# A planner that counts work on upper partitions, and activations with a scale per partition, as longer

## The chip, the cores and the metric

The kernel runs on one core of one Trainium2 chip. The metric is the device time of one execution in microseconds (us), the median over runs. The traces shown are of one profiled execution.

## What is computed

A trunk of two encoder layers over 512 tokens of 1024 features, in float32. Each layer is four residual steps, each followed by a layer norm:

```python
for i in range(DEPTH):                                   # DEPTH = 2
    y = swiglu(x, ffn_w_gate[i, 0], ffn_w_up[i, 0], ffn_w_down[i, 0])
    x = layer_norm(ALPHA * x + 0.5 * y, ln_g[i, 0], ln_b[i, 0])
    if i % 2 == 0:
        y = mixer_ab(x, ab_w_in[j], ab_w_out[j], ab_q_gain[j], ab_k_gain[j], ab_sink[j], ang_2d, ang_1d)
    else:
        y = mixer_c(x, c_w_in[j], c_w_out[j], c_rpb[j])
    x = layer_norm(ALPHA * x + y, ln_g[i, 1], ln_b[i, 1])
    y = memory_attn(x, mem, mem_w_q[i], mem_w_kv[i], mem_w_o[i])
    x = layer_norm(ALPHA * x + y, ln_g[i, 2], ln_b[i, 2])
    y = swiglu(x, ffn_w_gate[i, 1], ffn_w_up[i, 1], ffn_w_down[i, 1])
    x = layer_norm(ALPHA * x + 0.5 * y, ln_g[i, 3], ln_b[i, 3])
```

Mixer A/B (layer 0) has 8 heads A of dense attention and 8 heads B of attention in a window of 128 tokens to each side with a sink logit, all of width 64, and one output projection. Mixer C (layer 1) has 16 heads of width 64, each query attending to a neighbourhood of 8 x 16 tokens on a grid, with a bias by relative position. The memory step has 4 heads of width 256 over 256 memory tokens.

## The kernel before

The program is written as a plain sequence of operations, but is not issued in that order. A recorder (`Graph`) stands in for the five engines. It notes each operation with its engine, the operations it depends on, the buffers it uses, and `ns`, the time that `Graph.cost` thinks it takes. `Graph.emit` then runs a list scheduler, `Graph.plan`, twice: it keeps a clock for each engine and always issues the ready operation with the smallest key on the engine that is free first. In the first pass the key is the written order. From the first plan `deadlines` works out when each operation must start at the latest so that TensorE is not held up, and in the second pass these due times are the keys of VectorE, ScalarE and GpSimd. Nothing of these times reaches the chip; they set only the order of the instructions in each engine's queue. Every engine works off its queue in order. All operations are called from one helper, so nearly all instructions have the line L154 in the profile.

Buffers come in classes with a fixed number each, and a tile waits for its class to have one free: `t2` 14, `slab` 27, `raw` 2 (weights as they arrive), and the PSUM banks `a` 3 (projections, scores), `d` 2 (outputs), `t` 3 (transposes). Names in an order are the tile's class and running numbers.

Float32 products are made of two or three matmuls on a rounded high part and a remainder. So each operand is split: ScalarE writes the rounded copy (CAST, COPY or ACTIVATE), VectorE the difference (TENSOR_TENSOR or SCALAR_TENSOR_TENSOR).

In mixer A/B, `queries` splits transposed queries of two heads at a time: for each head, ScalarE writes the high part into one half of the partitions, and VectorE the remainder into the other half; both are 64 partitions high, and of each at least one operand lies on partitions 64 to 127 in VectorE's case, every second one in ScalarE's. For each of the 16 heads the loop then takes scores (`a`), their extreme (`mn`: TENSOR_REDUCE for A, an ISA instruction for B), the exponential with its sum (`l`), a RECIPROCAL, and `normalise`, a ScalarE copy whose scale is a column with a value per partition; the weights are transposed (`t`), split (`slab`), and multiplied with the values (`d`). Beside the last heads run the first half of the output projection (`x` += `d`) and the loads of its weights (`raw`<-ab_w_out).

In mixer C, `attend` moves the output's upper 64 partitions by a ScalarE COPY and adds on VectorE, 64 high, per head. Keys and queries are laid out by DMA (`slab`<-`t`), issued by SyncE in a queue which also loads weights (`raw`<-c_w_in). Each head is normalised in four pieces by `normalise`. The memory step uses `normalise` too.

`Graph.extent` gives the partitions that an operand covers, from its first to its last.

Of the kernel before, what the change touches and what calls it, by code (L numbers as in the profile page):

```python
# [65 lines left out]
class Graph:  # L66
# [45 lines left out]
    @staticmethod  # L112
    def cost(engine, method, out, ins, kw):
        n = 1
        for d in (out if method != "tensor_reduce" else ins[0]).ap[1:]:
            n *= d[1]
        wide = any(z.space == bass.MemoryType.PSUM for z in ins + [out]) if engine != "sync" else False
        if method == "dma_start":
            return 1200.0 if "accum_op" in kw else 600.0
        if engine == "tensor":  # L120
            return max(n / 2.4 + 14, 111)
        scalars = sum(1 for z in ins if z.ap[-1][1] == 1)
        if engine == "vector":
            if method == "tensor_scalar" and not wide:
                n = n / 2
            return n / 0.96 + 72 + 60 * scalars + 120 * (method == "scalar_tensor_tensor" and "accum_out" in kw)
        if engine == "scalar":
            return n / 1.2 + (55 if wide else 100) + 45 * scalars + 130 * ("accum_out" in kw)
        if n <= 8:
            return 270.0 if method == "tensor_scalar" else 200.0 if method != "tensor_tensor" else 390.0 + 157.0 * n  # L130
        if method == "memset":
            return n * 0.83 + 60
        dense = len(ins) == 2 and all(z.ap[-1][0] != 0 for z in ins)
        return n * (2.4 if dense else 1.7) + (70 if dense else 130)
# [1494 lines left out]
```

## Time and profile before

| | |
|---|---|
| runs | 2140.82, 2141.06, 2138.66 us; median 2140.82 |
| the profiled execution | 2139.44 us, span of its trace 2137.6 us |
| TensorE (PE) busy | 2116.6 us, 99% |
| weight loads (PEld) | 1886.3 us, 88% |
| VectorE (DVE) | 1725.9 us, 81% |
| ScalarE (ACT) | 1150.2 us, 54% |
| GpSimd (POOL) | 288.1 us, 13% |
| granted TensorE clock | 0.998 of full |

Times in a trace count from the start of the span. Mixer A/B lies at about 330 to 545 us, mixer C at about 1400 to 1600 us. A row of the timeline has the start, the length (of several instructions in a run, from the first start to the last end), the engine, the line, the operation, output and inputs, and how many; in brackets stands how long the engine was idle before it and what ended that. PE is TensorE's matmul, PEld its weight load, SPq the queue of SyncE. Matmuls are pipelined, so their rows overlap, and a row lasts longer than the step from one matmul to the next.

### The profile page before, as it was taken

Reading aid. Unit: us, or ns where it says so; the run is one execution under the profiler, and the core shown is the slowest. Engines: PE = TensorE matmul, PEld = TensorE weight load, DVE = VectorE, ACT = ScalarE, POOL = GpSimd, SP = SyncE. Lnnn points to the kernel's source line nnn. Section 1 sums busy time; section 2 is a strip of 40 time slices with the busy share of each in tenths; the row PEclk is TensorE's granted clock in tenths of the full one; section 3 lists DMA queues with packets and bytes.
Section 4 is the critical chain, followed back from the end, with each engine's and each line's share of the span. In section 5 each row is a group of like instructions: output and inputs, shape, how many; then the busy total and the mean of one; then the engine's idle time right before and its main releaser. Section 6 shows DMA issues by size and latency. Waiting matters only on the chain.

```text
span 2137.6 us, 33130 instructions
## 1 busy us (share of the span) xinstructions
PE 2116.6 (99%) x12904; PEld 1886.3 (88%) x12904; DVE 1725.9 (81%) x2460; ACT 1150.2 (54%) x1863; POOL 288.1 (13%) x379
## 2 busy tenths in 40 slices
PE   9999999999999999999999999999999999999997
PEld 7999988788888899999889999888888888999996
DVE  7789989888748879998879999865568479699997
ACT  5555543798446555445545455456665455445552
POOL 0001015310002000000200000412110011000003
PEclk9999999999999999999999999999999999999999
DMA  6566562003443247564445556255354333456551
GB/s 203 142 165 144 139 188 88 21 17 103 138 138 109 83 115 188 148 153 133 139 108 140 127 139 190 72 168 153 104 163 156 127 102 99 109 148 150 140 155 60
DMA packets 208861, 275.96 MB, mean 129 GB/s; under 512 B 10688, under 2 KB 151616, under 8 KB 208704
## 3 DMA queue, kind: packets, MB, share of 16 engines
q1 hardware_dynamic: 175904, 221.14, 33.3%
q0 software_dynamic: 32512, 52.44, 13.7%
q8 instruction: 102, 1.67, 0.3%
q14 instruction: 55, 0.45, 0.1%
q10 hardware_dynamic: 288, 0.26, 0.0%
HBM read 259.12 MB, written 4.19 MB: 123 GB/s over the span
## 4 chain that ended last, share of the span: by engine, by line
PE 72%; DMA 1%; DVE 1%; ACT 1%; SPq 0%; issue 0%; DVEq 0%; ACTq 0%
PE a L154 45%; PE d L154 15%; PE t L154 11%; DMA slab<-t 1%; DVE slab L154 1%; ACT t L154 0%; DVE x L154 0%; SPq L154 0%; DMA raw<-c_w_in 0%; DMA raw<-ab_w_out 0%; ACT slab L154 0%; DVE t L154 0%; DVE xl L154 0%; ACT junk L154 0%; DVEq L1625 0%
## 5 line engine op out<-in xcount | busy, mean ns | idle before, releaser
L154 DVE TENSOR_TENSOR slab<-slab,slab 128x1024 fp32r<-128x1024 f32 (+3 forms) x638 | 728.6, 1168 | 74.9 <-ACT slab L154 35.8
L154 ACT CAST slab<-slab 128x1024 fp32r<-128x1024 f32 (+2 forms) x498 | 472.3, 983 | 338.9 <-DVE slab L154 141.5
L154 PE MATMUL a<-slab,slab 128*128 128x256 f32 (+2 forms) x2456 | 570.5, 315 | 3.9 <-DMA slab<-t 3.4
L154 PE MATMUL a<-xh,slab 128*128 128x256 f32 (+2 forms) x2480 | 560.2, 315 | 0.1
L154 PEld LDWEIGHTS a<-slab,slab 128*128 128x128 f32 x2456 | 417.2, 191 | 37.4 <-issue 2.7
L154 PE MATMUL d<-slab,slab 128*128 128x512 f32 (+2 forms) x1856 | 447.8, 382 | 0.8 <-DVE slab L154 0.5
L154 PEld LDWEIGHTS a<-xh,slab 128*128 128x128 f32 x2480 | 416.9, 191 | 33.6 <-ACT slab L154 1.0
L154 PE MATMUL a<-xl,slab 128*128 128x256 f32 (+1 forms) x1240 | 390.6, 315 | 0.0
L154 PE MATMUL a<-raw,slab 128*128 128x256 f32 x2048 | 388.9, 283 | 0.9 <-DVE t L154 0.7
L154 PEld LDWEIGHTS d<-slab,slab 128*128 128x128 f32 x1856 | 329.2, 189 | 57.6 <-DVE slab L154 1.2
L154 PEld LDWEIGHTS a<-raw,slab 128*128 128x128 f32 x2048 | 328.1, 192 | 6.4 <-ACT slab L154 1.7
L154 PEld LDWEIGHTS a<-xl,slab 128*128 128x128 f32 x1240 | 236.6, 191 | 18.1
L154 PE MATMUL t<-slab,slab 128*128 128x512 f32 (+1 forms) x864 | 209.6, 383 | 0.0
L154 DVE TENSOR_TENSOR slab<-raw,slab 128x1024 fp32r<-128x1024 f32 (+2 forms) x132 | 158.6, 1220 | 23.7 <-ACT slab L154 23.6
L154 PEld LDWEIGHTS t<-slab,slab 128*128 128x128 f32 x864 | 151.4, 189 | 25.1
L154 DVE TENSOR_TENSOR slab<-t,slab 128x512 fp32r<-128x512 f32 (+2 forms) x211 | 131.4, 642 | 29.0 <-ACT slab L154 27.8
L154 ACT CAST slab<-raw 128x1024 fp32r<-128x1024 f32 (+1 forms) x124 | 123.0, 1021 | 25.7 <-PE a L154 9.0
L154 ACT CAST slab<-t 128x512 fp32r<-128x512 f32 (+2 forms) x211 | 114.4, 567 | 41.5 <-PE t L154 13.7
L154 DVE SCALAR_TENSOR_TENSOR x<-d,x 128x512 f32<-128x512 f32 x168 | 114.8, 686 | 18.8 <-PE d L154 18.0
L154 ACT COPY t<-a 128x512 f32<-128x512 f32 x96 | 56.3, 587 | 125.0 <-PE a L154 71.9
L154 POOL DMA_DIRECT2D slab<-ffn_w_down x40 | 47.7, 1193 | 313.5 <-DVE slab L154 291.2
L154 PE MATMUL a<-slab,xh 128*128 128x512 f32 (+1 forms) x272 | 79.8, 375 | 0.5 <-ACT xh L154 0.5
(126 smaller groups left out, 2138.2 us busy)
## 6 DMA issues: line engine op xcount, KB each, us to landing
slab<-ffn_w_gate SPq DMA_DIRECT2D x80, 512.0 KB
slab<-ffn_w_up SPq DMA_DIRECT2D x80, 512.0 KB
slab<-ffn_w_down SPq DMA_DIRECT2D x80, 512.0 KB
slab<-ffn_w_down POOLq DMA_DIRECT2D x40, 512.0 KB, 5.6
raw<-mem_w_kv SPq DMA_DIRECT2D x16, 1024.0 KB
slab<-t SPq DMA_DIRECT2D x96, 128.0 KB
slab<-ffn_w_gate POOLq DMA_DIRECT2D x16, 512.0 KB, 7.8
slab<-ffn_w_up POOLq DMA_DIRECT2D x16, 512.0 KB, 5.8
```

What stands on the lines that cost most here:

```text
L154: op.call = lambda: fn(*args, **kw)
```

## The change

`Graph.cost` gets two terms. `aside` adds 120 ns to an operation on VectorE or ScalarE of which any operand starts on a partition above 0. `scaled` adds 42 ns to a ScalarE activation whose scale is a tensor.

```diff
         scalars = sum(1 for z in ins if z.ap[-1][1] == 1)
+        aside = 120.0 * any(Graph.extent(z)[0] > 0 for z in ins + [out])
         if engine == "vector":
             if method == "tensor_scalar" and not wide:
                 n = n / 2
-            return n / 0.96 + 72 + 60 * scalars + 120 * (method == "scalar_tensor_tensor" and "accum_out" in kw)
+            return n / 0.96 + 72 + aside + 60 * scalars + 120 * (method == "scalar_tensor_tensor" and "accum_out" in kw)
         if engine == "scalar":
-            return n / 1.2 + (55 if wide else 100) + 45 * scalars + 130 * ("accum_out" in kw)
+            scaled = 42 * hasattr(kw.get("scale"), "tensor")
+            return n / 1.2 + (55 if wide else 100) + aside + 45 * scalars + 130 * ("accum_out" in kw) + scaled
```

The terms meet the operations of `queries` and `attend` named above, and every `normalise`. For an operation 512 wide that reads PSUM the plan's time goes from 605 to 725 ns on VectorE and from 482 to 602 on ScalarE; for a `normalise` of 512 columns it goes from 572 to 614 ns.

The program has the same instructions before and after; only their order on each engine differs, nearly all of it within mixer A/B from about 380 us on and mixer C. Line numbers move from L154 to L156.

First place, head A, near 439 to 446 us. On VectorE, before: `slab_790` are the half-high remainders of queries, `mn_782` and `mn_786` the extremes of scores, `slab_794` the split of a transposed bank, `slab_824` that of a weight.

```order
L154 SCALAR_TENSOR_TENSOR slab_790_871<-t_789_870,slab_790_871 64x512 x2
L154 TENSOR_REDUCE mn_782_863<-a_781_862 128x1
L154 TENSOR_REDUCE mn_786_867<-a_785_866 128x1
L154 RECIPROCAL l_776_857<-l_776_857 128x1
L154 RECIPROCAL l_780_861<-l_780_861 128x1
L154 RECIPROCAL l_784_865<-l_784_865 128x1
L154 TENSOR_TENSOR slab_791_872<-d_758_839,slab_791_872 128x512
L154 RECIPROCAL l_788_869<-l_788_869 128x1
L154 TENSOR_TENSOR slab_794_875<-t_793_874,slab_794_875 128x512
```

And now, the same stretch of VectorE:

```order
L156 TENSOR_REDUCE mn_782_863<-a_781_862 128x1
L156 SCALAR_TENSOR_TENSOR slab_790_871<-t_789_870,slab_790_871 64x512
L156 TENSOR_REDUCE mn_786_867<-a_785_866 128x1
L156 SCALAR_TENSOR_TENSOR slab_790_871<-t_789_870,slab_790_871 64x512
L156 TENSOR_TENSOR slab_791_872<-d_758_839,slab_791_872 128x512
L156 RECIPROCAL l_776_857<-l_776_857 128x1
L156 RECIPROCAL l_780_861<-l_780_861 128x1
L156 RECIPROCAL l_784_865<-l_784_865 128x1
L156 RECIPROCAL l_788_869<-l_788_869 128x1
L156 TENSOR_TENSOR slab_824_905<-raw_822_903,slab_823_904 128x1024
L156 TENSOR_TENSOR slab_794_875<-t_793_874,slab_794_875 128x512
```

The pair of half-high operations is parted, a reduce goes ahead of it, and the weight's subtraction comes before that of the bank, 12 rows earlier than it was. On ScalarE the weight's cast (slab_823<-raw_822) likewise goes 9 rows forward, ahead of the normalises and the bank's cast; on TensorE two score matmuls (a_805, a_809) go ahead of the four transposes of t_799.

Second place, head B, near 503 to 506 us, on TensorE before: `t_1030` and `t_1032` are transposes of normalised weights (`t2`), `a_1036` to `a_1044` scores of a later head, `d_1052` an output.

```order
L154 MATMUL t_1032_1113<-ident_1_78,t2_987_1068 128x128
L154 MATMUL t_1032_1113<-ident_1_78,t2_991_1072 128x128
L154 MATMUL a_1036_1117<-slab_858_939,slab_1025_1106 128x256
L154 MATMUL t_1032_1113<-ident_1_78,t2_995_1076 128x128
L154 MATMUL a_1036_1117<-slab_858_939,slab_1025_1106 128x256
L154 MATMUL a_1040_1121<-slab_858_939,slab_1025_1106 128x384 x2
L154 MATMUL a_1044_1125<-slab_858_939,slab_1025_1106 128x384 x2
L154 MATMUL d_1052_1133<-slab_1029_1110,slab_763_844 128x256
```

And now:

```order
L156 MATMUL t_1032_1113<-ident_1_78,t2_987_1068 128x128
L156 MATMUL t_1032_1113<-ident_1_78,t2_991_1072 128x128
L156 MATMUL a_1036_1117<-slab_858_939,slab_1025_1106 128x256 x2
L156 MATMUL a_1040_1121<-slab_858_939,slab_1025_1106 128x384 x2
L156 MATMUL a_1044_1125<-slab_858_939,slab_1025_1106 128x384 x2
L156 MATMUL t_1032_1113<-ident_1_78,t2_995_1076 128x128
L156 MATMUL d_1052_1133<-slab_1029_1110,slab_763_844 128x256
```

Five score matmuls move ahead of the transpose of t2_995. On ScalarE, four casts (slab_1029 to slab_1035) and the normalise of t2_995 move ahead of four exponentials (t2_1013, 1009, 1017, 1021); on VectorE the x operation (x3<-d_1027) moves ahead of the reciprocal l_997, which that normalise needs.

Third place, mixer C, near 1492 us, on TensorE before: `a_2670` to `a_2674` are scores that read the keys `slab_2634` brought by DMA, `d_2679` is the output of the head before.

```order
L154 MATMUL a_2672_2753<-slab_2634_2715,slab_2597_2678 128x256
L154 MATMUL a_2670_2751<-slab_2634_2715,slab_2597_2678 128x192
L154 MATMUL a_2672_2753<-slab_2634_2715,slab_2597_2678 128x256
L154 MATMUL a_2674_2755<-slab_2634_2715,slab_2597_2678 128x256 x2
L154 MATMUL d_2679_2760<-slab_2642_2723,slab_2573_2654 128x256
L154 MATMUL d_2679_2760<-slab_2642_2723,slab_2573_2654 128x2x128 x2
```

And now:

```order
L156 MATMUL d_2679_2760<-slab_2642_2723,slab_2573_2654 128x256 x2
L156 MATMUL a_2672_2753<-slab_2634_2715,slab_2597_2678 128x256
L156 MATMUL d_2679_2760<-slab_2642_2723,slab_2573_2654 128x2x128
L156 MATMUL a_2670_2751<-slab_2634_2715,slab_2597_2678 128x192
L156 MATMUL a_2672_2753<-slab_2634_2715,slab_2597_2678 128x256
L156 MATMUL a_2674_2755<-slab_2634_2715,slab_2597_2678 128x256 x2
L156 MATMUL d_2679_2760<-slab_2642_2723,slab_2573_2654 128x2x128
```

Two output matmuls move ahead of the second a_2670. On VectorE, the subtraction slab_2695<-raw_2691 moves six rows back. On SyncE's queue one load (raw_2682<-c_w_in) moves behind four key transfers, earlier in the stage.

## The prediction

> **What bounds the kernel now.** I read the page first, then the waits of TensorE, then busy time by stage, and last the single rows around each hole on TensorE.
>
> ```profile
> PE 2116.6 (99%) x12904; PEld 1886.3 (88%) x12904; DVE 1725.9 (81%) x2460; ACT 1150.2 (54%) x1863; POOL 288.1 (13%) x379
> ```
>
> TensorE is busy for 2116.6 of 2137.6 us: all that any order could win here is some 21 us, 1%. The waits of TensorE, over the whole span, say which holes there are:
>
> ```profile
> PE a L154 <- DMA slab<-t: 3.4, 9, 1.2
> ...
> PE t L154 <- DVE slab L154: 1.1, 3, 0.5
> PE t L154 <- ACT t L154: 0.9, 1, 0.9
> ```
>
> The first line (total, times, longest) is mixer C, scores that wait for keys brought by DMA. The others are the attention heads of mixer A/B, transposes waiting for VectorE to empty a PSUM bank, or for a normalised score. The change moves rows in these two stages, and otherwise only swaps neighbours. Busy time by stage (us, then each engine's busy us):
>
> ```profile
> 400.00:465.00 65.00, 63.95 (x344) 51.41 (x343) 53.86 (x127) 61.83 (x136) 8.76 (x19) 1.00 0.03 9
> 465.00:545.00 80.00, 77.62 (x445) 66.25 (x444) 66.15 (x176) 67.00 (x164) 7.44 (x28) 1.00 0.31 87
> 1430.00:1550.00 120.00, 116.55 (x731) 103.30 (x731) 65.69 (x167) 82.87 (x209) 27.69 (x65) 1.00 0.52 136
> ```
>
> The columns are PE, PEld, DVE, ACT, POOL. TensorE is idle for 1.05, 2.38 and 3.45 us: 6.9 us in all. ScalarE (61.83 of 65) is nearly full in the first: there, an order that wastes ScalarE time costs TensorE soon.
>
> **Is the plan's new price right?** The change adds no instruction; it alters what the plan believes. By form, durations show no upper-partition charge (mean ns at the end):
>
> ```profile
> L154 ACT CAST slab<-d 128x512 fp32r<-128x512 f32 x16 | 9.4, 585 | 11.0 <-PE d L154 10.9
> L154 ACT COPY t<-d 64x512 f32<-64x512 f32 x16 | 9.3, 582 | 2.7 <-PE d L154 2.4
> ```
>
> ```profile
> L154 DVE SCALAR_TENSOR_TENSOR slab<-d,slab 128x512 f32<-128x512 f32 x32 | 22.0, 687 | 0.6
> ...
> L154 DVE SCALAR_TENSOR_TENSOR slab<-t,slab 64x512 fp32r<-64x512 f32 x14 | 9.6, 688 | 3.1 <-ACT slab L154 2.9
> ```
>
> The spacing does show it. Rows that run without a break, on VectorE and then on ScalarE:
>
> ```profile
> 437.23 1.39 DVE L154 SCALAR_TENSOR_TENSOR slab<-t,slab 64x512 fp32r<-64x512 f32 x2 [0.50 <-ACT slab L154]
> 438.65 1.29 DVE L154 TENSOR_REDUCE mn<-a 128x1 f32<-128x512 f32 x2
> ```
>
> ```profile
> 436.00 1.20 ACT L154 ACTIVATE slab<-t 64x512 fp32r<-64x512 f32 x2 [0.59 <-PE t L154]
> ...
> 441.20 1.34 ACT L154 ACTIVATE t<-t,l 128x512 f32<-128x512 f32 x2
> 442.42 1.56 ACT L154 CAST slab<-t 128x512 fp32r<-128x512 f32 x3
> ```
>
> Two reduces take 1.29 us, about twice 0.69 less an overlap of 0.09: a step of 0.60. The two half-height operations overlap by nothing: a step of 0.70, and the reduce behind them also starts only at 438.65, 0.03 after 438.62. The plan said 0.605 for such an operation and now says 0.725; the trace says 0.70. On ScalarE the half-height step is 0.61 (1.20 less 0.59) against 0.48 for casts ((1.56 less 0.60)/2); the plan said 0.482, now 0.602. A normalise with a scale per partition steps by 0.61 (441.20, two, 442.42); the plan said 0.572, now 0.614. All three new prices are nearer to the trace than the old ones. So the plan should put fewer operations where their inputs come late.
>
> [...]
>
> The order after does split pairs: half-height operations on VectorE stand in 33 groups where they stood in 30. At 0.10 us for each extra lost overlap (0.70 less 0.60) that is up to +0.3 us on VectorE.
>
> **The sum, place by place.** First the hole at 443.79, in head A:
>
> ```profile
> 439.38 0.69 ACT L154 ACTIVATE t<-a,mn 128x512 f32<-128x512 f32 x1 [1.38 <-DVE mn L154]
> ...
> 442.30 0.95 PE L154 MATMUL a<-slab,slab 128*128 128x512 f32 x3
> 443.04 1.29 DVE L154 TENSOR_TENSOR slab<-t,slab 128x512 fp32r<-128x512 f32 x2 [1.53 <-ACT slab L154]
> 443.79 0.66 PE L154 MATMUL t<-ident,t 128*128 128x128 f32 x4 [0.54 <-DVE slab L154]
> ...
> 446.25 1.05 ACT L154 CAST slab<-raw 128x1024 fp32r<-128x1024 f32 x1
> ```
>
> ScalarE's exponential stood 1.38 us behind the two half-height operations and a reduce. In the new order that reduce (mn_782) goes ahead of the pair, so the exponential can start 1.4 us sooner (two steps of 0.70). But the weight cast of 446.25 is pulled ahead of the bank's cast (442.42), which takes back 0.95 (1.05 less the usual 0.10 overlap): 0.45 left; VectorE's 1024-wide subtraction is pulled ahead of 443.04 too, into 1.53 us of idle time. And two score matmuls, a_805 and a_809, of 0.235 each ((0.95 less 0.48)/2), now run ahead of the waiting transposes. 0.45 and 0.47 against a listed 0.54: the hole should close. Take −0.6, with −0.7 and +1.0 (the weight cast comes where nothing hides it) as the ends.
>
> The rest of 400 to 465 (1.05 less 0.54, 0.51 us listed) are small holes of the same kind near 404, 424 and 460, for which the new order also moves one to six matmuls forward. A listed hole is shorter than the time lost, as the next fence shows (0.25 each). Five such holes: 0.51 + 5 × 0.25 = 1.76. I take half, −0.9, ends 0 and −1.76.
>
> The largest hole in 465 to 545, in head B:
>
> ```profile
> 502.69 1.22 DVE L154 TENSOR_TENSOR slab<-raw,slab 128x1024 fp32r<-128x1024 f32 x1
> 503.34 0.36 PE L154 MATMUL a<-slab,slab 128*128 128x256 f32 x1
> 503.83 0.15 DVE L154 RECIPROCAL l<-l 128x1 f32<-128x1 f32 x1
> 504.02 0.69 DVE L154 SCALAR_TENSOR_TENSOR x<-d,x 128x512 f32<-128x512 f32 x1
> 504.08 0.51 ACT L154 ACTIVATE t<-t,l 128x256 f32<-128x256 f32 x1 [0.58 <-DVE l L154]
> 504.65 0.33 PE L154 MATMUL t<-ident,t 128*128 128x128 f32 x1 [0.94 <-ACT t L154]
> ...
> 508.61 1.02 ACT L154 ACTIVATE t<-t,l 128x256 f32<-128x256 f32 x2 [0.94 <-DVE l L154]
> ```
>
> A transpose waits for a normalise, it for a reciprocal, and that for the 1.22 us weight subtraction ahead of it. From 503.34 to 504.65 are 1.31 us for a matmul that steps by 0.12 (the row of 1488.68 below: (0.63 less 0.28)/3): 1.19 us are lost, 0.25 more than the row lists. The new order puts five matmuls ahead of that transpose: one of 256 columns and four of 384, 0.12 + 4 × 0.17 (in proportion to columns) = 0.8 us. Against it, VectorE's x operation of 504.02 (0.69) goes ahead of the reciprocal. Take −0.6, ends −1.0 and +0.3. The remaining listed idle time is 2.38 − 0.94 − 0.7 at the very end of the stage (below) = 0.74, in some four holes: 0.74 + 4 × 0.25 = 1.74; half, −0.9.
>
> Mixer A/B ends at a load, and what is won before might be lost there:
>
> ```profile
> 522.91 1.25 SPq L154 DMA_DIRECT2D raw<-ab_w_out  x2
> ...
> 530.42 1.99 ACT L154 CAST slab<-raw 128x1024 fp32r<-128x1024 f32 x2 [2.59 <-DMA raw<-ab_w_out]
> ```
>
> The load is issued when VectorE has finished with its buffer; that work stands behind transposes of the same chain, so it comes forward with TensorE, and the hole at the stage's end stays. One of the four casts of that buffer is put four rows later, behind casts that wait for TensorE: at most its step, 0.48, and nothing if VectorE's four subtractions of 0.60 each set the pace. I take +0.15.
>
> Mixer C:
>
> ```profile
> 1488.25 0.59 PE L154 MATMUL a<-slab,slab 128*128 128x192 f32 x3 [1.21 <-DMA slab<-t]
> 1488.68 0.63 PE L154 MATMUL d<-slab,slab 128*128 128x256 f32 x4
> ...
> 1492.30 0.47 PE L154 MATMUL a<-slab,slab 128*128 128x192 f32 x2 [0.22 <-DMA slab<-t]
> ```
>
> ```profile
> 1441.88 0.37 SPq L154 DMA_DIRECT2D raw<-c_w_in  x1
> 1442.35 2.39 SPq L154 DMA_DIRECT2D slab<-t  x4
> ...
> 1492.72 0.92 SPq L154 DMA_DIRECT2D raw<-c_w_in  x2
> 1505.46 9.72 SPq L154 DMA_DIRECT2D slab<-t  x12
> ```
>
> The holes end when keys land, and no key transfer comes much earlier. So only matmuls moved from behind the last hole of a group to ahead of it count. At 1492.30 they are two of 0.12 (−0.24), at the group near 1538 three (−0.36), near 1443 seven against a hole of about 0.35 (−0.35): −0.95, ends 0 and −1.6. A subtraction that frees a raw buffer is put six rows later, so SP's loads of 1492.72 slip by 2 us or so; SP does nothing more until 1505.46: cost nothing, unless it slips by over 12 us. One more weight load goes behind four key transfers, which step by about 0.6 (2.39/4); the rows give it no consumer near, so 0. That, and the swaps of neighbours elsewhere, the last output among them, I put at 0.
>
> Sum: −0.6 − 0.9 − 0.6 − 0.9 − 0.95 + 0.15 + 0.3 = −3.5 us. After both stages TensorE has no hole of this kind, so this reaches the end. Against the profiled execution, 2139.44, that is 2135.9; it lies 1.4 under the median of the runs (2140.82), so I predict 2137.3. From no change, 0.2% (4.3 us) is about what a measurement of this kernel can tell.
>
> **Rivals.**
> - *All holes fill.* The listed 6.9 us less the 0.7 that hangs on the load and the 2.5 that hang on late keys leave 3.7, with 0.25 for each of some ten holes 6.2: 2134.6. For it: the prices fit three rows. Against: the keys, and the reciprocal still behind the 1.22.
> - *Nothing of note.* Matmuls put ahead of a hole are then missing behind it, and in mixer A/B the head is paced by ScalarE, 61.83 of 65: within 1.5 us of 2140.8. Against it: in 500 to 510 ScalarE does wait, 0.58 and 0.94 us in the rows.
> - *Slower: exponentials too late.* In the new order four exponentials of head B are put behind four casts and a normalise that wait for TensorE. These are 4 × 0.4 less overlaps and 0.4, about 1.7 us. ScalarE's wait at 508.61 covers 0.94; beyond that each such head loses 0.76, and the order does alike near 475, 482 and 490: four heads, +3.0; with the weight cast at 443 unhidden (+1.0), no hole filled and the parted pairs (+0.3), 2145. It decides where exponentials slip by more than 0.94 us.
>
> **Numbers.** The forecast (−1.5 to −5.5) 0.52; all fill 0.15; nothing 0.19; slower 0.14. The range from 2132.5 to 2144 leaves out most of the last case's far end and little else; the likeliest case alone is 2135.3 to 2139.3. Faster by over 0.2% comes from the second and a fifth of the first: 0.26. Slower by that is over half of the last: 0.08. The rest, 0.66, can't be told from no change.
>
> **What would show it.** TensorE's idle in 400 to 465 falls below 0.6 us, and the hole near 443.8 is gone; the one near 504.6 shrinks to half. Scores' waits for slab<-t stay at 2.5 to 3.4 us. Durations by form stay as they are. It is wrong if waits of TensorE for ScalarE's t or slab appear in mixer A/B that were not there, or if the idle time near 531 grows by as much as is won before.

## The result and the profile after

The changed kernel takes 2135.51 us (median of 9 runs, 2133.87 to 2137.15) against 2140.55 us before (9 runs, 2138.65 to 2142.34). The ratio is 0.9978, 95% interval 0.9969 to 0.9987: faster by 5.0 us by the medians, by 0.22% by the ratio. 2137.3 was predicted, within 2132.5 to 2144. The profiled execution has a span of 2132.1 us.

The first line of the page, and the stages (stretch, length, then busy us of PE, PEld, DVE, ACT, POOL, granted clock, DMA share, GB/s):

```profile
PE 2114.9 (99%) x12904; PEld 1885.2 (88%) x12904; DVE 1724.7 (81%) x2460; ACT 1150.5 (54%) x1863; POOL 286.8 (13%) x379
```

```profile
400.00:465.00 65.00, 64.66 (x354) 52.62 (x353) 54.76 (x132) 63.07 (x138) 8.77 (x19) 1.00 0.04 9
465.00:545.00 80.00, 79.27 (x457) 67.86 (x456) 68.39 (x175) 66.92 (x162) 6.52 (x29) 1.00 0.31 87
1430.00:1550.00 120.00, 118.18 (x748) 104.84 (x747) 67.49 (x165) 81.86 (x202) 28.37 (x64) 1.00 0.51 138
```

Each engine does the same work as before, to within 2 us. TensorE's idle time falls from 1.05 to 0.34, from 2.38 to 0.73 and from 3.45 to 1.82 us: 4.0 of the 5.5 us by which the two spans differ. The rest doesn't show as idle time, since a matmul's row outlasts its step (0.28 us against 0.12 in the prediction's rows), so that a late start is in part covered by the row before. So I use a second measure below, the *lost time*: for every matmul its step to the next, less the median step of matmuls of its width in the same trace, summed over a stage. From 400 to 545 us it falls from 9.74 to 6.16 us, from 1400 to 1600 from 8.26 to 6.10, and elsewhere it differs by less than 0.2 in any stage; over the whole span it falls by 5.4 us.

What TensorE still waits for in these stages (total, times, longest):

```profile
PE a L156 <- DMA slab<-t: 1.7, 2, 0.9
...
PE d L156 <- DVE slab L156: 0.7, 1, 0.7
...
PE a L156 <- ACT t L156: 0.3, 1, 0.3
```

The waits of transposes for VectorE's slab (1.1) and ScalarE's t (0.9) are gone altogether. In head A, where the hole of 443.79 was, the timeline now reads:

```profile
437.22 0.68 ACT L156 ACTIVATE t<-a,mn 128x512 f32<-128x512 f32 x1
...
441.39 1.41 PE L156 MATMUL a<-slab,slab 128*128 128x512 f32 x5
441.82 1.29 DVE L156 TENSOR_TENSOR slab<-t,slab 128x512 fp32r<-128x512 f32 x2 [0.48 <-ACT slab L156]
...
442.64 0.38 PE L156 MATMUL t<-ident,t 128*128 128x128 f32 x2
```

The exponential that waited 1.38 us for its reduce follows the one before it at once. Score matmuls fill the time until VectorE has emptied the bank, near 442.5, and the transposes behind have no listed wait (0.54 before).

In head B, where TensorE lost 1.19 us at 504.65:

```profile
500.80 1.18 PE L156 MATMUL a<-slab,slab 128*128 128x256 f32 x6
501.05 0.15 DVE L156 RECIPROCAL l<-l 128x1 f32<-128x1 f32 x1
...
501.40 0.52 ACT L156 ACTIVATE t<-t,l 128x256 f32<-128x256 f32 x1
...
501.97 0.33 PE L156 MATMUL t<-ident,t 128*128 128x128 f32 x1
```

Score matmuls fill the time up to 501.97. The lost time there is 0.16 us. ScalarE's four exponentials and the normalises behind them:

```profile
504.29 0.61 ACT L156 ACTIVATE t<-t,mn 128x385 f32<-128x385 f32 x1
...
505.38 1.92 ACT L156 ACTIVATE t<-t,l 128x256 f32<-128x256 f32 x4
```

The last of the exponentials runs until about 505.4 and the first normalise follows with no wait (0.94 before). They were put later, and no wait follows in the rows.

### The profile page after: what moved, and what is told of

It reads as the page before. It is cut to its first block, busy times and chain, and to the rows that moved or that the text cites. A ratio compares the mean times of both kernels' runs of the same rounds, so it can differ in the third digit from the quotient of the medians.

```text
span 2132.1 us, 33129 instructions
## 1 busy us (share of the span) xinstructions
PE 2114.9 (99%) x12904; PEld 1885.2 (88%) x12904; DVE 1724.7 (81%) x2460; ACT 1150.5 (54%) x1863; POOL 286.8 (13%) x379
## 4 chain that ended last, share of the span: by engine, by line
PE 90%; DVE 1%; ACT 1%; DMA 1%; issue 0%; SPq 0%; DVEq 0%; ACTq 0%
PE a L156 55%; PE d L156 21%; PE t L156 14%; DVE slab L156 1%; DMA slab<-t 1%; ACT t L156 1%; ACT slab L156 0%; DVE x L156 0%; DMA raw<-ab_w_out 0%; DVE t L156 0%; SPq L156 0%; DVE xl L156 0%; ACT junk L156 0%; DVEq L1627 0%; DVE nmu L156 0%
## 5 line engine op out<-in xcount | busy, mean ns | idle before, releaser
L156 DVE TENSOR_TENSOR slab<-slab,slab 128x1024 fp32r<-128x1024 f32 (+3 forms) x638 | 728.6, 1168 | 74.3 <-ACT slab L156 36.0
L156 ACT CAST slab<-slab 128x1024 fp32r<-128x1024 f32 (+2 forms) x498 | 472.3, 982 | 339.5 <-DVE slab L156 146.0
L156 PE MATMUL a<-slab,slab 128*128 128x256 f32 (+2 forms) x2456 | 568.8, 314 | 2.2 <-DMA slab<-t 1.7
L156 PE MATMUL a<-xh,slab 128*128 128x256 f32 (+2 forms) x2480 | 560.0, 315 | 0.1
L156 PEld LDWEIGHTS a<-slab,slab 128*128 128x128 f32 x2456 | 417.0, 190 | 35.6 <-issue 1.7
L156 PE MATMUL d<-slab,slab 128*128 128x512 f32 (+2 forms) x1856 | 447.1, 381 | 0.8 <-DVE slab L156 0.7
L156 PEld LDWEIGHTS a<-xh,slab 128*128 128x128 f32 x2480 | 416.7, 191 | 33.6 <-ACT slab L156 1.1
L156 PE MATMUL a<-xl,slab 128*128 128x256 f32 (+1 forms) x1240 | 390.1, 315 | 0.0
L156 PE MATMUL a<-raw,slab 128*128 128x256 f32 x2048 | 388.8, 283 | 1.0 <-DVE t L156 0.8
L156 PEld LDWEIGHTS d<-slab,slab 128*128 128x128 f32 x1856 | 328.8, 189 | 57.3 <-DVE slab L156 1.7
L156 PEld LDWEIGHTS a<-raw,slab 128*128 128x128 f32 x2048 | 327.8, 192 | 6.6 <-ACT slab L156 1.8
L156 PEld LDWEIGHTS a<-xl,slab 128*128 128x128 f32 x1240 | 236.4, 191 | 18.2
L156 PE MATMUL t<-slab,slab 128*128 128x512 f32 (+1 forms) x864 | 209.5, 383 | 0.0
L156 DVE TENSOR_TENSOR slab<-raw,slab 128x1024 fp32r<-128x1024 f32 (+2 forms) x132 | 157.5, 1213 | 26.8 <-ACT slab L156 26.6
L156 PEld LDWEIGHTS t<-slab,slab 128*128 128x128 f32 x864 | 151.3, 189 | 25.2
L156 DVE TENSOR_TENSOR slab<-t,slab 128x512 fp32r<-128x512 f32 (+2 forms) x211 | 131.5, 642 | 26.6 <-ACT slab L156 25.8
L156 ACT CAST slab<-raw 128x1024 fp32r<-128x1024 f32 (+1 forms) x124 | 122.9, 1021 | 25.7 <-PE a L156 8.8
L156 ACT CAST slab<-t 128x512 fp32r<-128x512 f32 (+2 forms) x211 | 114.5, 566 | 40.7 <-PE t L156 13.2
L156 DVE SCALAR_TENSOR_TENSOR x<-d,x 128x512 f32<-128x512 f32 x168 | 114.9, 686 | 17.4 <-PE d L156 16.7
L156 ACT COPY t<-a 128x512 f32<-128x512 f32 x96 | 56.4, 587 | 124.8 <-PE a L156 71.9
L156 POOL DMA_DIRECT2D slab<-ffn_w_down x40 | 47.7, 1193 | 313.5 <-DVE slab L156 290.9
L156 PE MATMUL a<-slab,xh 128*128 128x512 f32 (+1 forms) x272 | 79.8, 374 | 0.5 <-ACT xh L156 0.5
```

The costliest lines, as they stand in the source:

```text
L156: op.call = lambda: fn(*args, **kw)
```

## The experiments

Four theories were set against each other. *Truer prices*: the plan gains to the extent that its prices agree with the trace. *One term*: only the half-high operations matter. *Any stir*: the order of a greedy planner is a draw, and any change of prices draws again. And, from the ninth run on, *room*: any price that makes VectorE and ScalarE look slower makes the plan put more matmuls ahead of a possible wait, true or not. All times:

| kernel | median us (runs) | before, same chip | ratio, 95% interval | lost 400:545 | lost 1400:1600 |
|---|---|---|---|---|---|
| before | 2140.55 (9) | | | 9.74 | 8.26 |
| changed | 2135.51 (9) | 2140.55 | 0.9978, 0.9969 to 0.9987 | 6.16 | 6.10 |
| only the 120 ns | 2137.33 (11) | 2140.52 | 0.9984, 0.9976 to 0.9993 | 7.51 | 9.29 |
| only the 42 ns | 2137.60 (11) | 2140.52 | 0.9986, 0.9977 to 0.9995 | 7.60 | 7.89 |
| mixer A/B only | 2137.07 (11) | 2140.52 | 0.9982, 0.9973 to 0.9990 | 6.47 | 10.58 |
| mixer C only | 2139.57 (11) | 2140.52 | 0.9994, 0.9985 to 1.0003 | 9.72 | 7.12 |
| signs turned | 2140.53 (11) | 2140.90 | 0.9998, 0.9990 to 1.0007 | 10.47 | 8.08 |
| half: 60 and 21 ns | 2138.11 (11) | 2140.90 | 0.9986, 0.9977 to 0.9995 | 7.95 | 7.85 |
| double: 240 and 84 ns | 2137.18 (11) | 2140.90 | 0.9983, 0.9974 to 0.9992 | 7.23 | 5.15 |
| charge for a change of partition | 2133.42 (5) | 2140.90 | 0.9969, 0.9956 to 0.9981 | 6.35 | 5.37 |
| extra on other operations | 2137.06 (11) | 2140.95 | 0.9986, 0.9977 to 0.9995 | 7.69 | 8.04 |
| changed, again | 2135.75 (11) | 2140.95 | 0.9977, 0.9968 to 0.9986 | 6.34 | 8.47 |
| change of partition, again | 2133.46 (5) | 2140.95 | 0.9966, 0.9953 to 0.9978 | 6.37 | 6.11 |
| before, again | 2141.22 (1) | | | 9.69 | 8.81 |

The lost time is of one trace each, in us. In the last column, four traces (only the 120 ns, mixer A/B only, changed again, before again) hold 1.5 to 1.6 us each that are not a wait for keys: for 3.4 us TensorE runs at half its clock there (granted 0.50, last section).

**One term at a time.**

```diff
-            scaled = 42 * hasattr(kw.get("scale"), "tensor")
+            scaled = 0
```

> Only the 120 ns for upper partitions is counted, the 42 ns for a scale per partition is not. Theory of truer prices (each price that comes nearer to the trace fills some holes): about two thirds of the gain of 5.0 us, -3 us, since two of the three prices are right. One-term theory (the half-high operations are all that matters): the whole -5. Theory of any stir (an order of a greedy planner is a draw, and a change of prices draws again): anything from -5 to +4, with new holes on TensorE in places where there were none.

and, with the other term alone,

```diff
-        aside = 120.0 * any(Graph.extent(z)[0] > 0 for z in ins + [out])
+        aside = 0.0
```

> Only the 42 ns for a scale per partition is counted. Truer prices: about a third, -1.5 to -2 us. One-term theory: within 0.5 us of before. Any stir: anything from -5 to +4.

By time the first gives 3.2 us and the second 2.9, where 5.0 are got together. The one-term theory is out: by it the 42 ns alone were to give nothing, which their interval excludes. They did more than the third that was expected of them. Part of the gain comes with either term: the lost time from 400 to 545 us falls by 2.2 us with the first, by 2.1 with the second and by 3.6 with both.

In head B, idle time of TensorE in 465 to 545 us was 2.38 before, and is 0.73 with both. With the 120 ns alone it is 2.04:

```profile
465.00:545.00 80.00, 77.96 (x445) 66.86 (x444) 67.14 (x173) 65.41 (x161) 7.56 (x29) 1.00 0.31 87
```

and with the 42 ns alone 1.81:

```profile
465.00:545.00 80.00, 78.19 (x449) 67.14 (x448) 66.85 (x174) 66.93 (x162) 6.53 (x29) 1.00 0.29 80
```

By idle time the terms seem to need one another here. By lost time, 5.71 before, 4.90 and 4.42 with one, 3.46 with both, they add up to within 0.2 us. What does need both are three holes: near 474, 488 and 503 us, 0.70, 0.25 and 0.46 us are lost with the 120 ns alone and 0.54, 0.38 and 0.65 with the 42 ns alone, and at most 0.18 with both.

**One stage at a time.** A flag is set while one mixer is recorded, and both terms are multiplied by it.

```diff
-        aside = 120.0 * any(Graph.extent(z)[0] > 0 for z in ins + [out])
+        aside = 120.0 * Graph.PRICED * any(Graph.extent(z)[0] > 0 for z in ins + [out])
...
-            scaled = 42 * hasattr(kw.get("scale"), "tensor")
+            scaled = 42 * Graph.PRICED * hasattr(kw.get("scale"), "tensor")
```

> Both terms count for operations of mixer A/B alone. By the lost time on TensorE in the two traces, read from start to start, mixer A/B gave 3.4 us and mixer C 2.0. If the stages do not meet: -3.4 us, TensorE's holes in 400 to 545 us as in the changed kernel, and those of 1430 to 1550 as before. If a gain in the first stage shifts the loads of the later one, this run and the next do not add up to -5.4.

> Both terms count for operations of mixer C alone. If the stages do not meet: -2.0 us, with scores waiting for keys for 1.7 us in place of 3.4. The prediction had put mixer C at -0.95: if that holds, the rest is a shift that came from mixer A/B.

By time mixer A/B gives 3.45 us, as its lost time had said. Mixer C gives 0.95, the number of the prediction, but its interval, −3.2 to +0.6 us, holds both none and the 2.0 read from the traces; in its trace scores wait 2.7 us for keys, between the 3.4 of before and the 1.7 that were foretold. Together that is 4.4 of 5.0 us, and the intervals are too wide to say whether the rest is more than noise. Mixer A/B's stages are reproduced by the run with A/B alone:

```profile
400.00:465.00 65.00, 64.65 (x354) 52.61 (x353) 54.78 (x132) 63.10 (x138) 8.79 (x19) 1.00 0.03 9
465.00:545.00 80.00, 79.23 (x455) 67.63 (x454) 68.20 (x175) 66.59 (x162) 6.53 (x29) 1.00 0.30 87
1430.00:1550.00 120.00, 115.07 (x720) 102.73 (x719) 64.96 (x160) 79.75 (x198) 27.94 (x62) 0.99 0.50 129
```

Idle time 0.35 and 0.77 where the changed kernel has 0.34 and 0.73. But mixer C, in the order of before, is idle for 4.93 us and not 3.45. Either a shift comes over from mixer A/B, or the transfers vary. So both kernels were profiled once more:

> The kernel before, profiled once more. With the kernel whose prices changed in mixer A/B alone, scores in mixer C waited 4.9 us for keys in place of 3.4, in the order of before. If that is variation of the transfers: this trace differs from the first by about as much, 1 us or more, in mixer C, and by less than 0.3 us in mixer A/B. If it is a shift that came from mixer A/B: 3.4 again.

> The changed kernel once more, beside the one that charges a change of partition, on one chip. Mixer A/B alone gave -3.4 and mixer C alone -1.0 us: -4.4 if they add, -5.0 as measured. In its trace the holes of mixer A/B should stand as in the first trace (3.4 us less than before), since its order and all its inputs are the same; those of mixer C may differ by up to 2 us if the time at which keys land varies from one execution to another.

The kernel before, again, and then the changed one, again:

```profile
400.00:465.00 65.00, 63.91 (x345) 51.30 (x344) 53.67 (x126) 61.88 (x136) 8.74 (x19) 1.00 0.04 9
465.00:545.00 80.00, 77.64 (x445) 66.28 (x444) 66.15 (x176) 67.38 (x164) 7.25 (x27) 1.00 0.31 87
1430.00:1550.00 120.00, 116.86 (x732) 104.14 (x730) 64.83 (x170) 83.34 (x213) 28.48 (x66) 0.99 0.53 138
```

```profile
400.00:465.00 65.00, 64.65 (x351) 52.50 (x350) 54.50 (x130) 63.08 (x138) 8.76 (x19) 1.00 0.04 9
465.00:545.00 80.00, 79.23 (x456) 67.70 (x455) 68.09 (x177) 66.94 (x163) 6.52 (x29) 1.00 0.30 87
1430.00:1550.00 120.00, 116.82 (x731) 104.27 (x730) 64.82 (x160) 80.14 (x201) 27.04 (x62) 0.99 0.51 136
```

In mixer A/B the idle times repeat: 1.09 and 2.36 (1.05 and 2.38), 0.35 and 0.77 (0.34 and 0.73). In mixer C they do not: 3.14 for 3.45, and 3.18 for 1.82 in the changed kernel. The lost time there is 8.26 and 8.81 in the order of before, 6.10, 8.47 and (mixer C only) 7.12 in the new one. Of the 8.81 and the 8.47, 1.6 and 1.5 us belong to the stretch at half clock; without it they are 7.2 and 7.0. So the second pair differs by 0.2 us where the first differed by 2.2, and the first pair overstated mixer C's part. Before's idle time differs from one trace to the other by 0.3, less than the 1 us that variation was to show; the changed kernel's by 1.4 us. A shift from mixer A/B into mixer C isn't excluded for the 4.93, but an unchanged program varies by nearly as much.

**Wrong prices and other sizes.** The signs turned, half and double:

```diff
-        aside = 120.0 * any(...)
+        aside = -120.0 * any(...)
...
-            scaled = 42 * hasattr(...)
+            scaled = -42 * hasattr(...)
```

> Both terms with the sign turned: half-high operations count 120 ns shorter, scaled activations 42 ns shorter, so the plan is wrong by twice as much as before. Truer prices: slower than before by 2 to 6 us, with more and longer waits of TensorE in mixer A/B and C. Any stir: a draw like any other, within 4 us of before and faster as likely as slower.

> 60 and 21 ns. The prices lie between those of before and the changed ones (an upper operation of 512 on VectorE 665 ns, against a step of 700 in the trace). Truer prices: between, -2 to -4 us. Any stir: -5 to +4, with no order among 0, half, whole and double.

> 240 and 84 ns: upper operations count 845 ns on VectorE against 700 in the trace. Truer prices: worse than the changed kernel, -3 to +1 us against before. Any stir: -5 to +4.

The turned signs cost nothing in time, and the slower run that truer prices foretold did not come. Room, which was set up later, would have had it slower too. In the trace they do harm, but little: lost time in mixer A/B 10.47 for 9.74, and transposes wait longer for VectorE's slab, 2.8 us in place of 1.1:

```profile
PE t L156 <- DVE slab L156: 2.8, 6, 0.7
```

Over the five sizes −1, 0, ½, 1, 2 the lost time in mixer A/B, where traces repeat, is 10.47, 9.74, 7.95, 6.16, 7.23: least at the prices that agree with the trace. By time −1 and 0 are level, ½, 1 follow in that order, and the double price comes between ½ and 1, with intervals that overlap. Its 3.7 us are a little more than the truer prices foretold for it (3 at most), and its runs spread from 2133.71 to 2140.51, so that its median says little. For any stir there is too much order in this; that it is a greedy draw on top is not excluded, since no changes of price at random were tried.

**The same amounts on other operations.** The prices of before, and 120 ns more for a reduce, 42 ns more for an exponential with a sum.

```diff
-            return n / 0.96 + 72 + 60 * scalars + ...
+            return n / 0.96 + 72 + 120 * ("reduce" in method) + 60 * scalars + ...
...
-... + 130 * ("accum_out" in kw)
+... + 172 * ("accum_out" in kw)
```

> The prices of before, with 120 ns more for every reduce on VectorE and 42 ns more for every exponential with a sum on ScalarE: the same amounts as the change, put on other operations of the same heads, for which the trace shows no such time (a reduce of 512 steps by 0.60 us, and the old price was 605 ns). A new theory, room (any price that makes VectorE and ScalarE look slower makes the plan put more matmuls ahead of what TensorE waits for, whether it is true or not): -3 to -6 us, like the changed kernel. Truer prices: none or slower, -1 to +4 us. Any stir: -5 to +4.

It is faster than before by 3.9 us by the medians, 3.0 by the ratio, 0.9986 (the changed kernel on the same chip: 5.2 and 4.9): what room foretold, and not what truer prices did. In mixer A/B 2.05 us of lost time go (9.74 to 7.69), where the true prices take 3.58. From 400 to 465 us that is 1.0 for 1.3, from 465 to 545 it is 1.0 for 2.25. The idle time of the two stretches:

```profile
400.00:465.00 65.00, 64.50 (x352) 52.69 (x351) 54.91 (x133) 63.73 (x140) 8.74 (x20) 1.00 0.03 9
465.00:545.00 80.00, 77.74 (x446) 67.14 (x445) 67.06 (x173) 65.94 (x161) 6.95 (x29) 1.00 0.31 87
```

0.50 for 1.05 in the first stretch, but 2.26 for 2.38 in the second. Of head B's three holes that only both true terms together closed, two stay (0.98 us lost at 474.85, 0.53 at 488.55) and the third is less than half of what it was (0.49 at 503.70, 1.19 before).

**A charge where the trace has it.** In the prediction's rows the full-high reduce behind a half-high operation started late too. In the changed kernel, where pairs are parted, VectorE shows this at every change in mixer A/B, here in head A:

```profile
436.55 0.68 DVE L156 SCALAR_TENSOR_TENSOR slab<-t,slab 64x512 fp32r<-64x512 f32 x1
437.25 0.69 DVE L156 TENSOR_REDUCE mn<-a 128x1 f32<-128x512 f32 x1
437.97 0.69 DVE L156 SCALAR_TENSOR_TENSOR slab<-t,slab 64x512 fp32r<-64x512 f32 x1
438.69 0.69 DVE L156 TENSOR_TENSOR slab<-d,slab 128x512 fp32r<-128x512 f32 x1
439.30 0.34 DVE L156 RECIPROCAL l<-l 128x1 f32<-128x1 f32 x4
```

Steps of 0.70, 0.72 and 0.72, and then 0.61 from one full-high operation to the next. The same holds for all of the changed kernel's operations of 512 columns from 330 to 545 us behind which VectorE's next one starts within 0.05 us: 0.70 to 0.72 at the 12 changes from half-high to full-high, 0.71 to 0.72 at the 5 changes back, and a median of 0.60 over the 112 steps from full-high to full-high. At each of these changes the step is the longer one, in either direction. So a plan was made that charges the change:

```diff
+            if e in self.PATIENT:
+                stop += 100.0 * any(place[e].get(m, p) != p for m, p in op.place)
+                place[e].update(reversed(op.place))
```

Here `op.place` lists the start partition of each input and of the output, reads and writes and the two memories apart; `aside` is 0 and the 42 ns stay.

> The plan charges no upper partitions; it adds 100 ns on VectorE or ScalarE wherever an operation starts reading or writing on another partition than the one before it on its engine (kept apart for PSUM and SBUF), as in the trace, where the full-high operation behind a half-high one starts late too. The 42 ns stay. Truer prices: as good as the changed kernel or better, -5 to -7 us, and on VectorE fewer parted pairs. Any stir: anything from -5 to +4.

> The plan that charges 100 ns for a change of partition, beside the changed kernel on the same chip. If truer prices are worth more: faster than that by 1 to 3 us, -6 to -7.5 against before. If its first time was luck of the chip: within 0.7 us of the changed kernel.

It is the fastest of all: 7.5 us under before both times, and on one chip 2.3 us under the changed kernel. Its ten runs lie between 2131.65 and 2134.30, and the changed kernel's twenty between 2133.68 and 2138.58. The intervals of the ratios against before overlap. In mixer A/B it loses as much as the changed kernel (6.35, 6.37); it parts pairs less, 31 groups on VectorE for 33. What the traces show of the gain lies in mixer C: 5.37 and 6.11 us lost against 6.10 and 8.47, of which 1.5 are the stretch at half clock. Without that stretch it is 0.8 us on average; where the rest of the 2.3 us comes from is not shown. SyncE there does the following, in the changed kernel and then in this one:

```profile
1473.87 3.24 SPq L156 DMA_DIRECT2D raw<-c_w_in  x2
1477.22 9.18 SPq L156 DMA_DIRECT2D slab<-t  x12
```

```profile
1473.78 0.37 SPq L157 DMA_DIRECT2D raw<-c_w_in  x1
1476.51 4.95 SPq L157 DMA_DIRECT2D slab<-t  x8
1481.50 0.62 SPq L157 DMA_DIRECT2D raw<-c_w_in  x1
1483.77 2.57 SPq L157 DMA_DIRECT2D slab<-t  x4
```

A weight load stands behind eight key transfers that used to stand behind it, and the first keys go out at 1476.51 instead of 1477.22. That this is what made it faster was not tried by itself.

## Why the prediction was right

Its steps, one by one:

- *The prices agree with the trace, so holes fill.* Right in its outcome, and in mixer A/B borne out by the sizes and by the three holes of head B. As the only cause it is too much: extra time on operations that had none gave 3.0 to 3.9 us as well. That a plan which knows of less room leaves more is the reading that fits this; it was tried with one set of prices.
- *443.79, −0.6.* The lost time there, 0.71, is gone: −0.7. Both causes named are in the rows: the reduce ahead, and the matmuls in front of the transposes. Which of them closed it was not tried.
- *The rest of 400 to 465, −0.9.* The stretch went from 4.03 to 2.70 us lost, −1.33 with the hole of 443.79, so −0.6 for the rest. The term was too large. One hole grew, from 0.28 to 0.56, at 458.71, where scores wait for an exponential to free their bank. In small, that is a sign of being wrong that the prediction named: a listed wait for ScalarE's t (0.3) where there was none, though it took little of the gain.
- *The hole at 504.65, −0.6.* −1.0 (1.19 to 0.16). The term was too small: the reciprocal did not slip, since VectorE reached its weight subtraction early enough.
- *The others in 465 to 545, −0.9.* The stretch went from 5.71 to 3.46, −2.25; without the hole of 504.65 −1.2. The term was too small by 0.3.
- *The end of mixer A/B.* Nothing won there and nothing lost, as said. The load comes forward with TensorE, and the hole stays (0.72 listed, before 0.18 and 0.53):

```profile
526.78 2.00 ACT L156 CAST slab<-raw 128x1024 fp32r<-128x1024 f32 x2 [1.85 <-DMA raw<-ab_w_out]
...
529.14 0.50 PE L156 MATMUL d<-slab,slab 128*128 128x512 f32 x1 [0.72 <-DVE slab L156]
```

- *Mixer C, −0.95.* −0.95 by time in the run with mixer C alone, within an interval of −3.2 to +0.6, so that the agreement is partly luck; the traces scatter too much to say better. Scores' waits for keys were to stay at 2.5 to 3.4 us: they are 1.7 in one trace of the changed kernel and 3.1 in the other. The weight loads that slipped on SyncE's queue show no cost.
- *Given back, +0.45.* 0.3 for parted pairs and 0.15 at the end were put down. The parted pairs are in the rows, VectorE's steps of 0.72, but stand in no hole of TensorE. This is half of what the sum had too little in mixer A/B; the other half is the terms, of which 504.65 was 0.4 too small. Mixer A/B was forecast at −2.55 with what was given back, and gave −3.45. With mixer C that makes −4.4; the last 0.6 up to 5.0 lies within the intervals.
- *The rivals.* Nothing of note (within 1.5 us) is out. By the change in time, −5.0, the forecast of −3.5 and the rival in which all holes fill, −6.2, are about equally far. The exponentials were put later, but with no wait behind them. The reciprocals came early enough that ScalarE's 0.94 us of idle time was used, and no wait stands behind them. Not all holes filled: 0.34 and 0.73 us of listed idle time are left in mixer A/B. Whether ScalarE, now busy for 63.07 of 65 us, is the next bound of heads A was not tried.

## What to carry to other kernels

Check a planner's prices against the step from one instruction to the next in the trace, not against durations: here the durations of half-high operations were the same to 3 ns and the steps differed by 0.1 us. Judge a new order by the waits in the stages that repeat from one execution to the next, and compare two profiles of the same program before reading a difference in a stage that waits for transfers; look at the granted clock there too. And try the same extra price where it is not true before crediting the truth: here more than half of the gain in mixer A/B came that way too.

## What the runs showed that was not expected

Holes in mixer C vary by over a microsecond in an unchanged program (1.82 and 3.18 us of idle time in the changed kernel's two traces), and in four of the fourteen traces the granted TensorE clock dips behind them. In the first trace of before and in the second, 1485 to 1500 us:

```profile
1485.00:1500.00 15.00, 13.04 (x92) 11.84 (x92) 6.70 (x25) 10.54 (x31) 4.40 (x9) 1.00 0.76 202
```

```profile
1485.00:1500.00 15.00, 13.12 (x83) 12.20 (x82) 7.07 (x23) 8.59 (x26) 4.60 (x11) 0.89 0.86 216
```

The idle time is alike, 1.96 and 1.88 us, but the clock is 1.00 in one and 0.89 in the other; the changed kernel's second trace has the same dip in the same 15 us, its first has none. The 0.89 is a mean. In the second trace of before, the clock is halved for 3.41 us and whole on either side:

```profile
1488.00:1491.41 3.41, 1.53 (x11) 1.16 (x9) 0.69 (x1) 1.53 (x2) 0.00 (x0) 1.00 1.04 227
1491.41:1494.82 3.41, 3.41 (x16) 3.41 (x17) 2.25 (x9) 2.30 (x9) 1.26 (x2) 0.50 0.85 185
```

Matmuls of 256 columns step by 0.213 us in the second stretch and by 0.120 elsewhere, and 1.6 us are lost there. Three more traces have a mean of 0.89 over 15 us in mixer C: the 120 ns alone and the changed kernel's second one from 1485 to 1500 us, and mixer A/B alone from 1535 to 1550. The runs of before scatter over 3.7 us (2138.65 to 2142.34), so one stretch is under half of that.

What sets it off is not shown. Just ahead of the halved stretch above, TensorE is idle for 1.88 of 3.41 us (3.41 less 1.53); in the first trace of before it is idle for 0.78 in the same 3.41 us, and the clock stays whole. But the idle time of 15 us does not tell the traces apart: from 1485 to 1500 us it is 1.65, 1.88 and 1.99 us in the three that dip there, and 1.96 in the first trace of before and 2.23 with mixer C alone, which both keep 1.00. With mixer A/B alone the 15 us of the dip have no idle time, and the 15 us ahead of them have 1.93. In the four executions with a dip mixer C lost 1.5 to 1.6 us beyond its holes; no kernel was made to find out why.
